# Five edits to the S5 scan stage of a one-core mixer kernel: scan tables, a fourth input buffer, a pinned state copy

## The chip, the cores and the metric

The kernel runs on one core of one Trainium2 chip. The metric is device time in microseconds (us) of that core, taken as the median over runs. Three runs of the kernel before gave 2406.51, 2410.03 and 6112.23 us; their median is 2410.03 us. The profile that is read below comes from one further execution, which took 2415.59 us.

## The reference, cut to what matters

The program is one inference step of a two-layer backbone over 2048 latent tokens and 128 context tokens (2176 together), width 1024. Layer 0 has two branches, gated linear attention and a bidirectional S5 state-space branch. Only the S5 branch is touched here. For each of 32 groups of 16 channels it runs a complex linear recurrence with 64 states, forward and backward in time, adds a skip term and applies a gelu:

```python
def s5_scan(u, lam_re, lam_im, log_dt, b_re, b_im, h0_re, h0_im):
    ...
    bu_re = jnp.einsum('blgh,gph->blgp', u, bb_re)
    bu_im = jnp.einsum('blgh,gph->blgp', u, bb_im)
    ...                                   # the start state h0 enters at token 0
    _, _, h_re, h_im = lax.associative_scan(combine, (a_re, a_im, bu_re, bu_im), axis=1)
    return h_re, h_im
# in even_mixer, forward and flipped, then
y5 = einsum(h_re, c_re) - einsum(h_im, c_im) + s5_d * uf
z = jax.nn.gelu(y5)
```

The final states of the context pass are an output too.

## The kernel before, in words

**Stages.** The kernel runs an input projection for part of the columns (`phase1`), then the S5 core woven with a dense projection (`s5_core` with `qz_pass`), then the S5 output gate with the backward half of the linear attention, the attention chunks, and the second layer. The change lies in the S5 core, which runs from about 286 to 705 us of the span.

**The S5 core.** The 2176 tokens are cut into 136 blocks of 16. A group g passes through three functions. `first(g)` loads its rows of a Toeplitz matrix (`tz`, by DMA on SP's queue), prepares small tables on ScalarE (ACT) and VectorE (DVE), and has GpSimd (POOL) build the weights `e`. `second(g)` transposes the input on TensorE (PE) into `U` (evicted by ACT, lines 694 to 696), transposes `e` into `winc` (702, 704), multiplies both into the block increments (708), and then runs the recurrence over blocks on DVE: lines 714 to 717 rotate the increments with the cosine and sine tables C and S, line 722 is one real scan per direction whose multiplicand is `go` (a decay per state, with zeros where the sequences meet), and lines 723 to 726 rotate back into H. `third(g)` copies the final state out of H (`s5fin`, line 731), multiplies U and H into the output on PE (735 to 738), applies the gelu on ACT (`zy`, 740) and stores it by two DMAs on ACT's queue (742).

**The tables.** `tables(g0)` serves the two groups g0 and g0+1. It copies 16 start columns on ACT (626 to 628) and doubles their length three times (m = 16, 32, 64): at each level four scalings on ACT (`tabw`, 637) and eight multiply-adds on DVE (641). The next level needs the result of the level before, so ACT and DVE hand over to each other three times. `tabs` has two buffers, so the tables of one pair can be written once the pair two before has been used up (its last reader is line 725). `go` is written by two ACT instructions for each group (675) into a ring of three buffers, U lies in a ring of three, which are zeroed at their edges by nine POOL memsets in `s5_setup` (396).

**The dense work.** Between the steps of the core, `qz_pass` gives PE blocks of 24 matmuls (100 to 102) into PSUM tiles named psD, of which there are two. ACT evicts each block (`fo`, line 814) and stores it by a DMA on its queue (815). As long as neither psD tile has been evicted, PE cannot begin the next block.

**What sets the order.** Each engine works off its queue in order. The order is written when the kernel is built, by a scheduler that plays the program on modelled durations: among the instructions whose inputs are there in the model, the one that stands first in the program text goes first. A tile whose buffers are all in use waits in the model for the release. The loop of the core is

```python
for g in range(33):
    if g < 27: weights(g + 5)
    if g < 31: first(g + 1)
    if g < 32: second(g)
    yield            # one dense block
    if g: third(g - 1)
    yield            # one dense block
```

Of the kernel before, what the change touches and what calls it, by code (L numbers as in the profile page):

```python
# [14 lines left out]
F32 = mybir.dt.float32  # L15
# [4 lines left out]
AF = mybir.ActivationFunctionType  # L20
# [28 lines left out]
class Kernel:  # L49
# [317 lines left out]
    def s5_setup(self, es):  # L367
# [24 lines left out]
        self.s5_U = []  # L392
        for j in range(3):
            u = c.tile([128, 2, 139], F32, name=f"s5U{j}")
            for z in (0, 129, 138):
                nc.gpsimd.memset(u[:, :, z : z + 1], 0.0)
            self.s5_U.append(u)
        V, G = nc.vector, nc.gpsimd
        with ExitStack() as e2:
            p = self.pool(e2, "s5s", 1, side="left")  # L400
            n = [0]
# [163 lines left out]
    def s5_core(self, es):  # L565
# [48 lines left out]
        late = self.pool(es, "s5l", 1, side="left")  # L614

        def tables(g0):

            t = p.tile([128, 2, 2, 2, 138], F32, name="tabs", tag="tabs", bufs=2)
            AA, BB = self.s5_AA, self.s5_BB
            for d in range(2):  # L620
                dg = slice(d * 32 + g0, d * 32 + g0 + 2)

                at = (lambda m, n: slice(m, m + n)) if d == 0 else (lambda m, n: slice(129 - m - n, 129 - m))
                rev = (lambda n: slice(0, n)) if d == 0 else (lambda n: slice(n - 1, None, -1))
                e = 128 if d == 0 else 0
                nc.scalar.copy(t[:, :, d, :, at(0, 16)], BB[:, :, dg, rev(16)].rearrange("p c g n -> p g c n"))
                nc.scalar.copy(t[:, :, d, :, e], AA[:, :, dg, 8].rearrange("p c g -> p g c"))
                nc.scalar.copy(t[:, :, d, :, 129:138], BB[:, :, dg, rev(9)].rearrange("p c g n -> p g c n"))
            four = [(d, gg) for d in range(2) for gg in range(2)]
            for m in (16, 32, 64):  # L630

                turn = lambda j, d, gg: AA[:, j, d * 32 + g0 + gg, m // 16 : m // 16 + 1]
                at = lambda d, a: slice(a, a + m) if d == 0 else slice(129 - m - a, 129 - a)
                ws = []
                for d, gg in four:
                    ws.append(p.tile([128, 2, 64], F32, name="tabw", tag="tabw", bufs=6)[:, :, 0:m])
                    nc.scalar.activation(ws[-1], t[:, gg, d, :, at(d, 0)], AF.Copy, scale=turn(1, d, gg))  # L637
                for (d, gg), w in zip(four, ws):
                    for j, op in ((0, OP.subtract), (1, OP.add)):
                        x = t[:, gg, d, j]  # L640
                        V.scalar_tensor_tensor(x[:, at(d, m)], x[:, at(d, 0)], turn(0, d, gg), w[:, 1 - j], op0=OP.mult, op1=op)  # L641
            return t
# [3 lines left out]
        quad, tabs, es, tzs, Hs, gos = {}, {}, {}, {}, {}, {}  # L646

        def first(g):
# [22 lines left out]
            if g % 2 == 0:  # L671
                tabs[g // 2] = tables(g)
            go = gos[g] = p.tile([128, 2, 138], F32, name="rgo", tag="rgo", bufs=3)
            for d in range(2):
                nc.scalar.activation(go[:, d], self.s5_go[:, d], AF.Copy, scale=self.s5_m16[:, d * 32 + g : d * 32 + g + 1])
# [11 lines left out]
        def second(g):  # L687

            ug, ut = quad[g // 4]
            U = self.s5_U[g % 3]  # L690
# [18 lines left out]
            C, S = (tabs[g // 2][:, g % 2, :, j] for j in range(2))  # L709
            go = gos.pop(g)  # L710
# [17 lines left out]
        def third(g):  # L728

            U, H, tz, ct = self.s5_U[g % 3], Hs.pop(g), tzs.pop(g), cts.pop(g)  # L730
            nc.scalar.copy(self.s5_fin[:, :, g], H.rearrange("p d c -> p (d c)")[:, 137:268:130])
# [8 lines left out]
            nc.scalar.activation(zy, py, AF.Gelu_apprx_tanh)  # L740
            for kt in range(2):
# [1057 lines left out]
```

## Time and profile before

| what | value |
|---|---|
| median of the runs | 2410.03 us |
| the profiled execution | 2415.59 us |
| its span, first to last instruction | 2413.7 us |
| mean granted TensorE clock over the span | 0.966 |
| PE busy over the span | 2268.3 us (94%) |
| DVE busy | 1659.3 us (69%) |
| ACT busy | 1042.7 us (43%) |
| POOL busy | 867.6 us (36%) |

The span is the time from the first to the last instruction; the profiled execution's own time is 1.9 us longer. PE, DVE, ACT and POOL are the four engines; PEld is PE's loading of weights, ACTq and SPq are the DMA issues on the queues of ACT and SP. An `L` with a number is a line of the kernel. In a row of waits, the instruction on the left had to wait for the one on the right of the arrow. In a row of the timeline, the bracket says how long the engine had been idle before the instruction and what ended that wait. The granted clock (PEclk) is 1.00 at 2.4 GHz and 0.50 at 1.2 GHz.

### The profile page before, as it was taken

How to read it: one execution, taken by the hardware profiler on the slowest of the kernel's cores; microseconds unless marked ns; L12 is line 12 of the kernel's file. 1: busy time of each engine (PE TensorE's matmuls, PEld its weight loads, DVE VectorE, ACT ScalarE, POOL GpSimd, SP SyncE). 2: the span in 40 equal slices, each digit the busy share in tenths (PEclk: the TensorE clock that was granted, in tenths of full speed). 3: DMA queues.
4: the chain of work that ended last, by engine and by line, in shares of the span. 5: the costliest groups of instructions: out<-in, count | busy, mean ns of one | idle time of the engine just before them, and what ended most of it. 6: DMA issues, size and time to landing. Idle time of an engine off the chain costs nothing.

```text
span 2413.7 us, 47276 instructions
## 1 busy us (share of the span) xinstructions
PE 2268.3 (94%) x17473; PEld 2108.3 (87%) x17473; DVE 1659.3 (69%) x3916; ACT 1042.7 (43%) x2533; POOL 867.6 (36%) x1348
## 2 busy tenths in 40 slices
PE   7999887888899987999999999999999997999998
PEld 4988787887897876888888999999999997999998
DVE  4997688888866776888887665565344336676765
ACT  3554644343544453455454432233122115565653
POOL 4127165566522227767674021111101102222221
PEclk9999988999999995999999999999999998999999
DMA  9765853343469873333333642245133223222221
GB/s 322 236 210 181 252 162 99 102 132 110 131 212 310 291 232 100 123 119 123 116 115 102 210 120 80 80 138 147 50 93 102 68 69 100 88 89 88 90 69 58
DMA packets 328040, 332.90 MB, mean 138 GB/s; under 512 B 43969, under 2 KB 274977, under 8 KB 327809
## 3 DMA queue, kind: packets, MB, share of 16 engines
q1 hardware_dynamic: 265312, 238.84, 33.1%
q0 software_dynamic: 14384, 48.65, 5.9%
q10 hardware_dynamic: 48112, 42.38, 5.4%
q8 instruction: 138, 2.26, 0.4%
q14 instruction: 94, 0.76, 0.1%
HBM read 223.57 MB, written 106.22 MB: 137 GB/s over the span
## 4 chain that ended last, share of the span: by engine, by line
PE 57%; DVE 8%; issue 4%; DMA 4%; ACT 2%; POOL 2%; SPq 0%; ACTq 0%; POOLq 0%; DVEq 0%
PE psD L100 7%; PE psW L100 7%; PE psW L101 7%; PE psW L102 7%; PE psD L102 7%; PE psD L101 7%; PE psP L1081 3%; PE psW L1510 2%; PE psW L1463 2%; DVE tabs L641 2%; PE psT L1498 2%; PE psP L1098 1%; PE psP L1096 1%; DMA wst<-in_w_in_o_dram 1%; DMA wst<-h_d 1%
## 5 line engine op out<-in xcount | busy, mean ns | idle before, releaser
L100 PE MATMUL psD<-slot,yT 128*128 128x256 f32 x1088 | 318.2, 293 | 1.9 <-ACT yT L1125 1.9
L102 PE MATMUL psD<-slot,yT 128*128 128x256 f32 x1088 | 314.1, 292 | 0.0
L101 PE MATMUL psD<-slot,yT 128*128 128x256 f32 x1088 | 310.7, 286 | 0.0
L101 PE MATMUL psW<-hq,slot 128*128 128x272 f32 x1024 | 293.0, 287 | 0.0
L102 PE MATMUL psW<-hq,slot 128*128 128x272 f32 x1024 | 292.9, 287 | 0.0
L100 PE MATMUL psW<-hq,slot 128*128 128x272 f32 x1024 | 289.1, 287 | 0.0
L100 PE MATMUL psD<-hq,slot 128*128 128x272 f32 x768 | 235.1, 308 | 46.8 <-ACT fo L814 45.8
L101 PE MATMUL psD<-hq,slot 128*128 128x272 f32 x768 | 230.0, 300 | 0.0
L102 PE MATMUL psD<-hq,slot 128*128 128x272 f32 x768 | 229.5, 300 | 0.0
L100 PEld LDWEIGHTS psD<-slot,yT 128*128 128x128 f32 x1088 | 208.1, 191 | 10.0 <-ACT yT L1125 2.0
L102 PEld LDWEIGHTS psD<-slot,yT 128*128 128x128 f32 x1088 | 205.8, 191 | 4.5 <-issue 2.2
L101 PEld LDWEIGHTS psD<-slot,yT 128*128 128x128 f32 x1088 | 208.1, 191 | 1.8
L100 PEld LDWEIGHTS psD<-hq,slot 128*128 128x128 f32 x768 | 151.8, 199 | 55.2 <-ACT fo L814 48.8
L102 PEld LDWEIGHTS psW<-hq,slot 128*128 128x128 f32 x1024 | 193.1, 189 | 0.0
L101 PEld LDWEIGHTS psW<-hq,slot 128*128 128x128 f32 x1024 | 192.5, 188 | 0.0
L100 PEld LDWEIGHTS psW<-hq,slot 128*128 128x128 f32 x1024 | 190.6, 188 | 0.0
L641 DVE SCALAR_TENSOR_TENSOR tabs<-tabs,s5A,tabw 128x16 f32<-128x16 f32 (+2 forms) x384 | 146.8, 447 | 24.9 <-ACT tabw L637 23.5
L101 PEld LDWEIGHTS psD<-hq,slot 128*128 128x128 f32 x768 | 152.1, 198 | 6.4 <-issue 4.7
L102 PEld LDWEIGHTS psD<-hq,slot 128*128 128x128 f32 x768 | 152.1, 198 | 1.0 <-issue 1.0
L1472 DVE CUSTOM_DVE_ANT_0 sc<-psW,amask,sink 128x512 f32<-128x512 f32 (+1 forms) x128 | 93.6, 732 | 84.7 <-PE psT L1498 76.2
L1007 ACT ACTIVATE arg<-arg 128x512 f32<-128x512 f32 x119 | 75.0, 631 | 143.6 <-POOL arg L1006 140.3
L1475 ACT ACTIVATE sc<-sc,nm 128x512 f32<-128x512 f32 (+1 forms) x128 | 90.9, 710 | 87.9 <-DVE nm L1474 74.8
(376 smaller groups left out, 6543.2 us busy)
## 6 DMA issues: line engine op xcount, KB each, us to landing
wst<-h_d SPq DMA_DIRECT2D x96, 272.0 KB
hq<-hl_d SPq DMA_DIRECT2D x40, 544.0 KB
hl_d<-ht POOLq DMA_DIRECT2D x17, 1024.0 KB, 6.7
wada<-in_w_ada_dram SPq DMA_DIRECT2D x32, 512.0 KB
h_d<-hf SPq DMA_DIRECT2D x17, 512.0 KB
x_d<-x ACTq DMA_DIRECT2D x17, 512.0 KB
h_d<-hf ACTq DMA_DIRECT2D x17, 512.0 KB
wst<-h_d SPq DMA_DIRECT2D x34, 256.0 KB
```

What stands on the lines that cost most here:

```text
L100: mm(out, lh, rh, start=start, stop=False)
L101: mm(out, lh, rl, start=False, stop=False)
L102: mm(out, ll, rh, start=False, stop=stop)
L641: V.scalar_tensor_tensor(x[:, at(d, m)], x[:, at(d, 0)], turn(0, d, gg), w[:, 1 - j], op0=OP.mult, op1=op)
L1007: nc.scalar.activation(arg, arg, AF.Exp, scale=0.0625)
L1081: nc.tensor.matmul(pv[:, hh, pr, :], ak[o : o + 64, pr, :], aq[o : o + 64, pr, :], start=True, stop=True)
L1096: nc.tensor.matmul(ot, qh[o : o + 64, 0, pr, :], sf[o : o + 64, pr], start=True, stop=False)
L1463: nc.tensor.matmul(out, r32(qs[:, j, h]), kk, start=j == 0, stop=j == 1)
L1472: V.tensor_tensor_reduce(sv, ps, mask, 1.0, sk[:, h : h + 1], op0=OP.add, op1=OP.max, accum_out=m)
L1475: nc.scalar.activation(sv, src, AF.Exp, bias=nm[:, h : h + 1], accum_out=sm[:, h : h + 1])
L1498: nc.tensor.transpose(pt[:, c, :], t[:, 128 * c : 128 * c + 128], self.ident)
L1510: nc.tensor.matmul(po[kv][:, j % 2], r32(VV[:, b, kv]), r32(t[:, x, :, c, :]), start=c + x == 0, stop=c + x == nb)
```

## The change

Five edits, all in the S5 core. (1) The tile of the tables gets a third plane that holds `go` for its pair of groups, written in `tables` by four ACT instructions ahead of the doubling; the ring of `go` buffers is gone. (2) `tables(g + 1)` is called in `first(g)` of odd g instead of `tables(g)` in `first(g)` of even g, so each call stands one group earlier in the program. (3) U has four buffers instead of three; they and their memsets move from `s5_setup` to the core. (4) The copy of the final state stands behind the gelu, and is pinned there: `keep_in_program_order` lets the scheduler put it on ACT's queue only behind the ACT instruction that stands before it in the program, which is the gelu. (5) `tabw` has four buffers instead of six.

```diff
-        self.s5_U = []
-        for j in range(3):
-            u = c.tile([128, 2, 139], F32, name=f"s5U{j}")
-            for z in (0, 129, 138):
-                nc.gpsimd.memset(u[:, :, z : z + 1], 0.0)
-            self.s5_U.append(u)
@@ s5_core
         late = self.pool(es, "s5l", 1, side="left")
+        self.s5_U = []
+        for j in range(4):
+            u = late.tile([128, 2, 139], F32, name=f"s5U{j}")
+            for z in (0, 129, 138):
+                nc.gpsimd.memset(u[:, :, z : z + 1], 0.0)
+            self.s5_U.append(u)
@@ tables
-            t = p.tile([128, 2, 2, 2, 138], F32, name="tabs", tag="tabs", bufs=2)
+            t = p.tile([128, 2, 2, 3, 138], F32, name="tabs", tag="tabs", bufs=2)
...
+            for d, gg in four:
+                j = d * 32 + g0 + gg
+                nc.scalar.activation(t[:, gg, d, 2], self.s5_go[:, d], AF.Copy, scale=self.s5_m16[:, j : j + 1])
...
-                    ws.append(p.tile([128, 2, 64], F32, name="tabw", tag="tabw", bufs=6)[:, :, 0:m])
+                    ws.append(p.tile([128, 2, 64], F32, name="tabw", tag="tabw", bufs=4)[:, :, 0:m])
@@ first
-            if g % 2 == 0:
-                tabs[g // 2] = tables(g)
-            go = gos[g] = p.tile([128, 2, 138], F32, name="rgo", tag="rgo", bufs=3)
-            for d in range(2):
-                nc.scalar.activation(go[:, d], self.s5_go[:, d], AF.Copy, scale=self.s5_m16[:, d * 32 + g : d * 32 + g + 1])
+            if g == 0:
+                tabs[0] = tables(0)
+            if g % 2 and g < 31:
+                tabs[g // 2 + 1] = tables(g + 1)
@@ second
-            U = self.s5_U[g % 3]
+            U = self.s5_U[g % 4]
...
-            C, S = (tabs[g // 2][:, g % 2, :, j] for j in range(2))
-            go = gos.pop(g)
+            C, S, go = (tabs[g // 2][:, g % 2, :, j] for j in range(3))
@@ third
-            U, H, tz, ct = self.s5_U[g % 3], Hs.pop(g), tzs.pop(g), cts.pop(g)
-            nc.scalar.copy(self.s5_fin[:, :, g], H.rearrange("p d c -> p (d c)")[:, 137:268:130])
+            U, H, tz, ct = self.s5_U[g % 4], Hs.pop(g), tzs.pop(g), cts.pop(g)
...
             nc.scalar.activation(zy, py, AF.Gelu_apprx_tanh)
+            self.tc.keep_in_program_order(nc.scalar.copy(self.s5_fin[:, :, g], H.rearrange("p d c -> p (d c)")[:, 137:268:130]))
```

## Rows read from the trace of the kernel before

**Rows 1.** Busy time by engine in two stretches: the S5 core, what follows.

```profile
300.00:705.00 405.00, 348.80 (x2588) 329.08 (x2587) 332.66 (x757) 175.19 (x594) 229.97 (x331) 0.92 0.44 130
705.00:755.00 50.00, 47.06 (x346) 40.11 (x345) 29.87 (x58) 26.85 (x62) 11.38 (x19) 0.97 1.00 303
```

**Rows 2.** Waits in 290 to 705 us: total us, times, longest us.

```profile
ACT tabw L637 <- DVE tabs L641: 59.8, 67, 4.0
PE psD L100 <- ACT fo L814: 45.8, 13, 5.6
ACT s5U L696 <- PE psW L736: 43.8, 14, 4.8
ACT s5fin L731 <- DVE rh L726: 41.3, 28, 4.3
DVE ra L714 <- PE psW L708: 32.1, 11, 4.8
ACT rgo L675 <- DVE rb L722: 25.7, 12, 5.1
```

**Rows 3.** Timeline of PE: five short stalls of the dense blocks.

```profile
394.94 0.39 PE L100 MATMUL psD<-hq,slot 128*128 128x272 f32 x1 [2.74 <-ACT fo L814]
...
448.14 0.39 PE L100 MATMUL psD<-hq,slot 128*128 128x272 f32 x1 [2.57 <-ACT fo L814]
...
500.09 0.39 PE L100 MATMUL psD<-hq,slot 128*128 128x272 f32 x1 [3.02 <-ACT fo L814]
...
551.68 0.39 PE L100 MATMUL psD<-hq,slot 128*128 128x272 f32 x1 [3.02 <-ACT fo L814]
...
605.09 0.39 PE L100 MATMUL psD<-hq,slot 128*128 128x272 f32 x1 [2.55 <-ACT fo L814]
```

**Rows 4.** Timeline of PE: five long stalls, the first and the last.

```profile
366.56 0.59 PE L100 MATMUL psD<-hq,slot 128*128 128x272 f32 x1 [5.63 <-ACT fo L814]
...
577.85 0.59 PE L100 MATMUL psD<-hq,slot 128*128 128x272 f32 x1 [5.53 <-ACT fo L814]
```

**Rows 5.** Timeline of ACT around the short stall of 448 us, and after it.

```profile
447.39 0.41 ACT L675 ACTIVATE rgo<-s5go,s5m 128x138 f32<-128x138 f32 x1 [4.37 <-DVE rb L722]
447.71 0.38 ACT L814 ACTIVATE fo<-psD 128x272 f32<-128x272 f32 x1
...
453.54 0.21 ACT L696 COPY s5U<-ugt 128x16 f32<-128x16 f32 x1 [3.23 <-PE psW L736]
454.00 0.40 ACT L740 ACTIVATE zy<-psW 128x274 f32<-128x274 f32 x1 [0.26 <-PE psW L738]
```

**Rows 6.** Timeline of ACT before the long stall that ends at 472.75 us.

```profile
459.16 0.20 ACT L731 COPY s5fin<-rh 128x2 f32<-128x2 f32 x1 [2.33 <-DVE rh L726]
...
460.00 0.71 ACT L675 ACTIVATE rgo<-s5go,s5m 128x138 f32<-128x138 f32 x2
...
470.58 0.73 ACT L637 ACTIVATE tabw<-tabs,s5A 128x128 f32<-128x128 f32 x2 [1.78 <-DVE tabs L641]
...
472.30 0.40 ACT L814 ACTIVATE fo<-psD 128x272 f32<-128x272 f32 x1 [0.99 <-DMA z_d<-zy]
```

**Rows 7.** Timeline of DVE in the same stretch.

```profile
457.42 0.77 DVE L725 TENSOR_TENSOR ra<-rb,tabs 64x276 f32<-64x276 f32 x1
...
460.95 6.97 DVE L641 SCALAR_TENSOR_TENSOR tabs<-tabs,s5A,tabw 128x16 f32<-128x16 f32 x12 [1.82 <-ACT tabw L637]
467.84 0.43 DVE L714 TENSOR_TENSOR ra<-tabs,psW 128x276 f32<-128x276 f32 x1
```

**Rows 8.** Busy time by engine right after that long stall (columns as in rows 1).

```profile
472.70:478.20 5.50, 5.45 (x25) 5.45 (x26) 3.15 (x10) 1.94 (x6) 0.00 (x0) 0.53 0.21 67
```

**Rows 9.** Views of two tiles, tabs and s5U: one line of each.

```profile
L641 DVE SCALAR_TENSOR_TENSOR tabs<-tabs,s5A,tabw x384: 220/275/1274, 288.4 to 672.5; 128x16 f32<-128x16 f32 x64, 128x32 f32<-128x32 f32 x64, 128x64 f32<-128x64 f32 x64
...
L396 POOL MEMSET s5U<- x9: 101/101/103, 65.5 to 65.8; 128x2 f32 x9
```

**Rows 10.** The smallest form of line 641, in 300 to 705 us.

```profile
L641 DVE SCALAR_TENSOR_TENSOR tabs<-tabs,s5A,tabw 128x16 f32<-128x16 f32 x120 | 57.3, 544 | 23.4 <-ACT tabw L637 23.3
```

In rows 1 and 8 the columns are the stretch and its length, then busy us (and instructions) of PE, PEld, DVE, ACT and POOL, the granted clock, the share of the DMA engines and GB/s. In rows 9 stand the count, min/median/max ns of one instruction, the first and last start, and the forms; in rows 10 busy us, mean ns of one, and the idle time before them.

More of the change, by code (lines that the diff above doesn't have):

```diff
@@ L625, in tables @@
                 e = 128 if d == 0 else 0
-                nc.scalar.copy(t[:, :, d, :, at(0, 16)], BB[:, :, dg, rev(16)].rearrange("p c g n -> p g c n"))
-                nc.scalar.copy(t[:, :, d, :, e], AA[:, :, dg, 8].rearrange("p c g -> p g c"))
-                nc.scalar.copy(t[:, :, d, :, 129:138], BB[:, :, dg, rev(9)].rearrange("p c g n -> p g c n"))
+                nc.scalar.copy(t[:, :, d, 0:2, at(0, 16)], BB[:, :, dg, rev(16)].rearrange("p c g n -> p g c n"))
+                nc.scalar.copy(t[:, :, d, 0:2, e], AA[:, :, dg, 8].rearrange("p c g -> p g c"))
+                nc.scalar.copy(t[:, :, d, 0:2, 129:138], BB[:, :, dg, rev(9)].rearrange("p c g n -> p g c n"))
             four = [(d, gg) for d in range(2) for gg in range(2)]
+            for d, gg in four:
+                j = d * 32 + g0 + gg
+                nc.scalar.activation(t[:, gg, d, 2], self.s5_go[:, d], AF.Copy, scale=self.s5_m16[:, j : j + 1])
             for m in (16, 32, 64):
@@ L635, in tables @@
                 for d, gg in four:
-                    ws.append(p.tile([128, 2, 64], F32, name="tabw", tag="tabw", bufs=6)[:, :, 0:m])
-                    nc.scalar.activation(ws[-1], t[:, gg, d, :, at(d, 0)], AF.Copy, scale=turn(1, d, gg))
+                    ws.append(p.tile([128, 2, 64], F32, name="tabw", tag="tabw", bufs=4)[:, :, 0:m])
+                    nc.scalar.activation(ws[-1], t[:, gg, d, 0:2, at(d, 0)], AF.Copy, scale=turn(1, d, gg))
                 for (d, gg), w in zip(four, ws):
@@ L645, in s5_core @@
         up = self.u_d[NLAT:NT, :].rearrange("(c t) (g h) -> c g t h", t=16, h=16)
-        quad, tabs, es, tzs, Hs, gos = {}, {}, {}, {}, {}, {}
+        quad, tabs, es, tzs, Hs = {}, {}, {}, {}, {}
         def first(g):
```

## The prediction

> **What bounds the kernel now.** I read first the busy times of the S5 core. In 405 us PE is busy for 348.8 and DVE for 332.7, ACT for only 175.2 [rows 1]. So neither PE (56.2 us idle) nor DVE (72.3 us idle) fills the stage, and all that a better order in it can give lies within these two figures. Then I read who waits. PE's idle time is nearly all of one kind: 45.8 us in 13 waits for `fo`, the eviction of a dense block by ACT [rows 2]. ACT is idle for more than half of the stage and still late with it, since it works off its queue in order and stands before instructions whose inputs are missing: `tabw` (59.8 us), the U copy (43.8), the final state's copy (41.3), `go` (25.7) [rows 2]. Last I read the timelines, to see which of these waits stands ahead of an `fo` that PE needs. PE's stalls have two shapes:
>
> - **Short**, five of them, 2.74, 2.57, 3.02, 3.02 and 2.55 us, together 13.90 us [rows 3]. ACT waits 4.37 us for an old scan to release a `go` buffer, and `fo` stands right behind that `go` [rows 5].
> - **Long**, five of 5.5 to 5.6 us [rows 4]. ACT goes through the `tabw` chain, waits 1.78 us for DVE's table work in the midst of it, then 0.99 us behind the gelu's DMA issues, and then comes `fo` [rows 6]. In the 5.5 us after such a stall PE's granted clock is 0.53, the level of 1.2 GHz [rows 8], so about 0.47 x 5.5 = 2.6 us more are lost each time.
>
> After both shapes PE brings the increments late, and DVE waits for them (32.1 us in 11 waits, rows 2). That is the same time seen from another engine, and I do not add it.
>
> **Part by part.**
>
> *`go` moves into the tables.* The 64 instructions stay, and so does their form; the wait for the scan goes. Their new buffer is that of the tables, whose copies wait for line 725 anyway. With the wait, the short stalls go, as `fo` is then first in line: -13.90 us. Bounds: 0, if another late instruction slides in ahead of `fo`; -13.9 at best. What is late next there is `winc`, whose inputs come from PE itself. On the other side, four `go` instead of two stand ahead of each doubling chain. Two take 0.71 us [rows 6], 0.3 to 0.4 each as they overlap, so the chain starts 0.6 us later. Where the chain holds up `fo` (the five long stalls) that costs 5 x 0.6 = +3.0 us.
>
> *The final state's copy behind the gelu.* The copy's wait stands in front of the tables' copies: these need line 725, which ends at 457.42 + 0.77 = 458.19, but the copy runs at 459.16 [rows 6, 7]. So the chain can start 0.97 us earlier, five times: -4.9 us. Behind the gelu the copy finds H long done and costs its 0.2 us. Bounds: 0, if the gelu now waits for H in its place, and -4.9. Together with the two more `go`: -1.9 us.
>
> *Four buffers for U.* ACT's wait for PE's line 736 goes (43.8 us in 14 waits), but behind it stands the gelu, which waits for line 738 of the same `third` and comes 0.26 us after [rows 5]. ACT is held to the same point, and meanwhile PE is busy with those very matmuls. I cost it at nothing; the cover is PE's own work. If the scheduler uses the freedom to bring increments forward, the gain is at most the part of DVE's 32.1 us that is not behind the short stalls, some 18 us; this end goes to the second rival. Twelve memsets instead of nine, at 0.1 us [rows 9], move on POOL's queue from 65 us to the start of the stage, behind POOL's DMA issues of the projection; the first U is written at 300 us. Nothing, or 1.2 us once if they come late.
>
> *Tables a group ahead.* They still have two buffers, and the copies already run within 2 us of the release: line 725 ends at 458.19, the `go` that follow the copies start at 460.00 [rows 6, 7]. Earlier in the program is therefore not earlier in time. What changes is rank: table work now comes before the `second` that it used to follow. In the long shape DVE ran lines 714 to 716 (three of 0.43 us) between twelve and twelve multiply-adds of the chain [rows 7], and ACT's wait of 1.78 us lay there. If the chain goes first, `fo` comes 1.3 us earlier five times, -6.5 us; if the modelled order stays, 0. I take half, -3.2.
>
> *`tabw` from six to four.* A level uses four, and each scaling of the next level needs the multiply-adds that free its predecessor's buffer. Nothing; where two tables overlap, at the start, one level's handover of four times the mean wait (59.8/67 = 0.9 us) or 3.6 us, once.
>
> *Given back.* POOL's 230 us of work then fall into a shorter stage, and DVE's multiply-adds are slow beside POOL: the smallest form takes 544 ns in the mean where the shortest took 220 [rows 9, 10]. A stage shorter by 18 us raises POOL's share from 57 to 59.5 in a hundred; if the further 2.5 in a hundred of DVE's 332.7 us ran at half pace, 8 us would be added, of which I take a quarter as on the path: +2.0 us, bounds 0 and 8.
>
> The Trainium skill says more on this (SBUF — State Buffer, section "Who interferes with whom"): a DVE instruction with two SBUF inputs and a GpSimd instruction that reads SBUF exclude each other, the later one blocking fully. By that rule the stage would be full already and the sum would be zero. The trace agrees only in part: DVE finished twelve multiply-adds in 6.97 us, and a full block would let none through beside a busy POOL. It stands as the first rival below.
>
> **Sum.** -13.9 - 1.9 - 3.2 + 2.0 = -17.0 us. Against the profiled execution (2415.6 us) that is 2398.6. This execution lies 5.6 us above the median of the runs (2410.0), so the median becomes **2393 us**. What follows the core is PE-bound at 47.1 of 50 us [rows 1], so I carry the gain to the end undiminished.
>
> **Rivals.**
>
> *The slack is taken up by DVE and POOL.* The waits leave ACT, but DVE's own chain lengthens as its work falls beside POOL's. For it: 544 against 220 ns. Against it: DVE is idle for 72 us. The give-back is then at its upper bound and the table terms at zero: -13.9 + 8 = -6, or 2404 us.
>
> *All of `fo`'s lateness goes.* With three of its four waits removed, ACT comes to every `fo` in time: 45.8 us, and 5 x 2.6 = 13 us of clock, -59 us, within DVE's 72.3 idle us: about 2352 us. Against it: the `tabw` wait, the greatest, is not touched. Half of the way is as likely as all of it, so I put this case at 2352 to 2375.
>
> *Slower: every pair takes the long shape.* With the tables ranked before `second`, ACT puts the whole chain, now with four `go`, ahead of `winc` and `fo` in both pairs of four groups, instead of in every other one. It decides from the point where `fo` stands behind the last `tabw` in the pairs that now have the short shape. Each short stall of 2.8 us becomes 5.5 + 2.6 = 8.1: 5 x 5.3 = +26.5 us, or 2437 us. With the remaining six of the 16 pairs at 8.1 too it would be +75 and 2485. For it: the wait on line 725 stays at the chain's head. Against it: of the chain itself nothing changes but its start, by 0.6 us.
>
> *The edits change nothing.* The tables are bound by their buffers, the U copy by the gelu, and another wait slides ahead of `fo`: 2410. This is near the first rival, and I count the two together.
>
> **How the numbers follow.** Forecast 0.52 (its own range, from the terms' bounds, 2380 to 2404), first rival with no change 0.23 (2402 to 2414), all lateness gone 0.12, slower 0.13. For 8 in 10 the range runs from 2358, which keeps about half of the good case, to 2428, which leaves out most of the slow one. The measurement tells about 2%, here 48 us, from no change. Faster by more than that (under 2362) needs most of the good case: 0.09. Slower by more (over 2458) needs the slow one in nearly all pairs: 0.05. The rest, 0.86, lies within.
>
> **What would show it.** Right: no wait for the scan in ACT's list any more; no stall of 2.5 to 3 us of PE on `fo`; waits for H gone from the state's copy, with the gelu's own wait for line 738 grown; the U copy no longer waiting for line 736; the `tabw` wait still near 60 us, and long stalls of about 5 us with a clock near 0.5 behind them. Wrong: more than ten stalls of PE on `fo`; a stage whose PE idle time stays at 56 us though the scan wait is gone; DVE's busy time in the stage above 340 us; an ACT wait on line 725 that has grown by what the others lost.

## The result, and the profile after

Four runs of the changed kernel have a median of 2384.03 us (2383.14 to 2391.86), three of the kernel before beside them 2410.03 (2406.51 to 2414.85). Two runs, one of the kernel before (6112.23 us) and one of only_pin below (3555.09), were in a much slower state and are in no median here. The ratio is 0.9888, 95% interval 0.9869 to 0.9907: faster by 26 us between the medians, 27 by the ratio, or 1.1%, which by the bound of 2% counts as within it. The forecast was 2393. It lay 9 us too high.

I cut both traces at the same four events: ACT's first write to a table, the transpose of the final state on PE (end of the core), the first matmul into psP (end of the next stage), and ACT's first `asq` (end of the third). All stages between these follow by name. The core took 417.6 us and takes 396.3 (-21.3), the next stage 198.9 and now 191.3 (-7.6), the third 472.4 and 470.9, the rest 1039.0 and 1037.3; the core starts 1.1 us later. The four differences and the start give the 30.9 us by which the span is shorter (2413.7 to 2382.8).

Busy time by engine of the kernel before, then of the changed kernel, in the core and in the next stage (columns as in rows 1):

```profile
285.89:703.53 417.64, 355.96 (x2633) 335.62 (x2631) 340.76 (x779) 187.97 (x630) 229.97 (x331) 0.92 0.46 134
...
703.53:902.43 198.90, 189.61 (x1420) 157.01 (x1417) 137.06 (x287) 99.64 (x231) 51.26 (x89) 0.99 0.85 274
```

```profile
286.97:683.31 396.34, 350.59 (x2656) 333.00 (x2655) 338.63 (x781) 182.82 (x634) 240.09 (x331) 0.93 0.48 142
683.31:874.60 191.29, 180.29 (x1396) 153.29 (x1393) 136.00 (x286) 98.01 (x228) 51.94 (x92) 0.99 0.88 285
```

In the core PE's idle time went from 61.7 to 45.8 us. The count of PE's instructions is the second thing to see: 23 more in the core, 24 fewer behind it. By tile they are 24 matmuls of a dense block (`psD` from `hq`), which the scheduler has drawn from the next stage into the core. So the two stages are best taken as one sum: 616.5 us before, 587.6 after, with 4053 and 4052 instructions. At the pace of the next stage before (189.6 us busy for 1420 instructions) the 24 are worth some 3.2 of its 7.6 us; this is an estimate.

Waits of the changed kernel in 280 to 690 us, which answer to [rows 2]:

```profile
ACT zy L740 <- PE psW L738: 62.8, 24, 9.3
...
ACT tabs L626 <- DVE ra L726: 30.9, 12, 7.6
...
ACT tabw L640 <- DVE tabs L644: 27.6, 31, 5.5
...
PE psW L737 <- DVE rh L727: 25.3, 10, 4.4
ACT s5U L698 <- PE psW L736: 24.9, 12, 5.4
PE psD L100 <- ACT fo L815: 9.0, 3, 6.1
DVE ra L715 <- PE psW L710: 7.5, 5, 3.0
```

Two waits of the kernel before that belong beside these, in 290 to 705 us:

```profile
ACT zy L740 <- PE psW L738: 11.6, 17, 3.1
...
ACT tabs L626 <- DVE ra L725: 4.9, 5, 1.5
```

PE's wait for `fo` has fallen from 45.8 to 9.0 us, and in its place stands a wait that the kernel before hardly had (0.5 us): 25.3 us for `H`, the result of the scans. ACT's waits for the scan and for `H` are gone, the gelu's has grown from 11.6 to 62.8, `tabw` has halved, and the tables' copies now wait 30.9 us for line 726 (the line 725 of before, 4.9 us there).

Timelines of the changed kernel, DVE first, then ACT, PE and POOL, in the stretch that answers to [rows 6, 7]:

```profile
398.37 6.61 DVE L644 SCALAR_TENSOR_TENSOR tabs<-tabs,s5A,tabw 128x16 f32<-128x16 f32 x22 [1.54 <-ACT tabw L640]
404.90 0.43 DVE L715 TENSOR_TENSOR ra<-tabs,psW 128x276 f32<-128x276 f32 x1
...
409.04 1.67 DVE L723 TENSOR_TENSOR_SCAN rb<-tabs,ra 128x138 f32<-128x138 f32 x2
...
411.46 0.44 DVE L725 TENSOR_TENSOR ra<-rb,tabs 64x276 f32<-64x276 f32 x1
...
412.39 0.45 DVE L727 TENSOR_TENSOR rh<-rh,ra 128x276 f32<-128x276 f32 x1
...
416.16 0.87 DVE L725 TENSOR_TENSOR ra<-rb,tabs 64x276 f32<-64x276 f32 x1
```

```profile
398.03 0.94 ACT L640 ACTIVATE tabw<-tabs,s5A 128x32 f32<-128x32 f32 x4
...
399.62 0.39 ACT L815 ACTIVATE fo<-psD 128x272 f32<-128x272 f32 x1
...
402.27 0.38 ACT L815 ACTIVATE fo<-psD 128x272 f32<-128x272 f32 x1
...
403.10 0.41 ACT L640 ACTIVATE tabw<-tabs,s5A 128x128 f32<-128x128 f32 x1
...
416.03 0.40 ACT L740 ACTIVATE zy<-psW 128x274 f32<-128x274 f32 x1 [9.32 <-PE psW L738]
```

```profile
412.89 0.82 PE L737 MATMUL psW<-rh,ct 128*128 128x137 f32 x2 [4.44 <-DVE rh L727]
```

```profile
399.25 1.26 POOL L577 TENSOR_TENSOR ct<-s5M,s5CY 128x272 f32<-128x272 f32 x2
402.94 1.32 POOL L578 TENSOR_TENSOR ct<-s5R,s5CX 128x272 f32<-128x272 f32 x2 [2.43 <-PE psW L738]
...
409.62 1.52 POOL L577 TENSOR_TENSOR ct<-s5M,s5CY 128x272 f32<-128x272 f32 x2
416.08 1.46 POOL L578 TENSOR_TENSOR ct<-s5R,s5CX 128x272 f32<-128x272 f32 x2 [4.93 <-PE psW L738]
```

Before, DVE did twelve multiply-adds of a chain, then `second`'s products, then the other twelve [rows 7]. Now it does 22 of the 24 first. Over the 16 passes, the five that were cut after twelve now run 24, 22, 24, 24 and 24 in a row; most of the others are still cut. ACT's chain of scalings takes 5.5 us (398.03 to 403.51), where it took 10.7 (460.61 to 471.31). One `fo` stood in the midst of the chain before, two stand in this one.

The chain needs the first 16 of the 24 multiply-adds, as the last eight, of its third level, feed no scaling. Busy time from the first to the end of the 16th (columns as in rows 1), in the kernel before, the changed one, and two kernels of the next section, only_ahead and ahead_u4:

```profile
460.95:470.81 9.86, 6.26 (x52) 6.04 (x51) 9.80 (x20) 3.70 (x13) 9.49 (x15) 1.00 0.14 42
```

```profile
398.37:402.43 4.06, 4.06 (x36) 4.06 (x35) 4.06 (x17) 3.56 (x13) 2.14 (x4) 1.00 0.08 30
```

```profile
403.39:408.23 4.84, 4.84 (x43) 4.84 (x42) 4.84 (x17) 3.87 (x15) 3.14 (x6) 1.00 0.02 8
```

```profile
454.67:462.24 7.57, 7.57 (x65) 7.56 (x63) 7.57 (x17) 4.24 (x15) 6.96 (x12) 1.00 0.18 56
```

So the 16 took 9.86 us with POOL busy for 9.49 of them, and now take 4.06 with POOL busy for 2.14: it pauses for 2.43 us, until PE's line 738 frees a buffer of `ct`. Of the 5.8 us between the two only 1.3 are the three products that no longer lie in between. The rest is that the multiply-adds themselves are shorter, as they are in few_pool below, where POOL has little to do.

But `second`'s products wait behind the 22, the scans behind the products, and PE stands 4.44 us for `H` at 412.89. The granted clock behind this stall is 0.50, the level of 1.2 GHz, as it was 0.53 behind a long stall of before [rows 8]:

```profile
412.80:418.30 5.50, 5.41 (x24) 5.41 (x25) 5.21 (x12) 0.48 (x2) 2.22 (x3) 0.50 0.17 49
```

### The profile page after: what moved, and what is told of

Same layout as the page of the kernel before. It is cut to its first block, busy times and chain, and to the rows that moved or that the text cites. A ratio compares the mean times of both kernels' runs of the same rounds, so it can differ in the third digit from the quotient of the medians.

```text
span 2382.8 us, 47320 instructions
## 1 busy us (share of the span) xinstructions
PE 2251.9 (95%) x17473; PEld 2101.3 (88%) x17473; DVE 1656.2 (70%) x3916; ACT 1035.6 (43%) x2533; POOL 879.1 (37%) x1351
## 3 DMA queue, kind: packets, MB, share of 16 engines
q1 hardware_dynamic: 265312, 238.84, 33.4%
## 4 chain that ended last, share of the span: by engine, by line
PE 61%; DVE 11%; DMA 4%; issue 4%; ACT 3%; POOL 2%; ACTq 0%; SPq 0%; POOLq 0%; DVEq 0%
PE psD L100 8%; PE psD L102 7%; PE psD L101 7%; PE psW L100 7%; PE psW L102 7%; PE psW L101 7%; DVE tabs L644 3%; PE psP L1082 3%; PE psW L1511 3%; PE psW L1464 2%; PE psT L1499 2%; PE psP L1099 1%; PE psP L1097 1%; DVE rb L723 1%; DMA wst<-in_w_in_o_dram 1%
## 5 line engine op out<-in xcount | busy, mean ns | idle before, releaser
L100 PE MATMUL psD<-hq,slot 128*128 128x272 f32 x768 | 232.6, 303 | 18.1 <-ACT fo L815 9.0
L102 PE MATMUL psD<-hq,slot 128*128 128x272 f32 x768 | 227.4, 296 | 0.0
L101 PE MATMUL psD<-hq,slot 128*128 128x272 f32 x768 | 226.7, 296 | 0.2 <-DVE hq L232 0.2
L100 PEld LDWEIGHTS psD<-slot,yT 128*128 128x128 f32 x1088 | 207.6, 191 | 10.7 <-ACT yT L1126 2.4
L100 PEld LDWEIGHTS psD<-hq,slot 128*128 128x128 f32 x768 | 149.7, 195 | 24.6 <-ACT fo L815 9.6
L101 PEld LDWEIGHTS psD<-hq,slot 128*128 128x128 f32 x768 | 149.5, 195 | 4.0 <-issue 3.5
L102 PEld LDWEIGHTS psD<-hq,slot 128*128 128x128 f32 x768 | 149.4, 195 | 2.5 <-issue 2.5
L644 DVE SCALAR_TENSOR_TENSOR tabs<-tabs,s5A,tabw 128x16 f32<-128x16 f32 (+2 forms) x384 | 117.6, 374 | 28.6 <-ACT tabw L640 27.4
```

What stands on the lines that cost most here:

```text
L100: mm(out, lh, rh, start=start, stop=False)
L101: mm(out, lh, rl, start=False, stop=False)
L102: mm(out, ll, rh, start=False, stop=stop)
```

## Experiments

One table for all. Times are medians; the ratio is to the kernel before, run beside each on the same chip (its medians there were 2409.0 to 2411.3 us); "two stages" is the core and the next one in the profiled execution; "chain" is the time from the first to the last `tabw` scaling, summed over the 16 passes of the tables.

| kernel | us | ratio, interval | core | two stages | third | PE on `fo` | PE on `H` | chain |
|---|---|---|---|---|---|---|---|---|
| before | 2410.03 | 1 | 417.6 | 616.5 | 472.4 | 45.8 | 0.5 | 153.6 |
| only_pin | 2401.90 | 0.9969 (0.9958 to 0.9981) | 413.3 | 604.6 | 474.0 | 41.6 | under 0.5 | 158.1 |
| only_u4 | 2403.09 | 0.9972 (0.9961 to 0.9982) | 406.8 | 602.8 | 471.4 | 37.7 | 1.1 | 151.3 |
| only_go | 2393.24 | 0.9935 (0.9923 to 0.9947) | 404.2 | 601.7 | 468.9 | 31.9 | 8.1 | 157.1 |
| only_ahead | 2391.55 | 0.9928 (0.9915 to 0.9941) | 390.8 | 587.6 | 481.3 | 11.5 | 21.1 | 133.2 |
| no_ahead | 2387.02 | 0.9894 (0.9878 to 0.9911) | 402.8 | 593.6 | 469.9 | 33.0 | 2.9 | 168.8 |
| no_go | 2385.02 | 0.9891 (0.9876 to 0.9906) | 397.7 | 589.7 | 472.4 | 18.1 | 17.3 | 139.2 |
| no_pin | 2390.59 | 0.9914 (0.9899 to 0.9929) | 390.6 | 586.1 | 480.2 | 9.5 | 26.0 | 122.9 |
| no_u4 | 2381.40 | 0.9883 (0.9868 to 0.9898) | 395.2 | 584.9 | 471.4 | 9.5 | 24.6 | 122.9 |
| ahead_pin | 2382.76 | 0.9898 (0.9880 to 0.9917) | 397.3 | 588.2 | 471.1 | 14.3 | 14.5 | 142.0 |
| ahead_u4 | 2404.25 | 0.9983 (0.9972 to 0.9993) | 409.2 | 605.6 | 471.1 | 42.5 | 1.8 | 137.6 |
| fin_dve | 2394.54 | 0.9950 (0.9934 to 0.9966) | 396.8 | 591.8 | 480.4 | 7.1 | 25.3 | 117.8 |
| few_pool | 2325.59 | 0.9661 (0.9647 to 0.9676) | 343.7 | 535.9 | 471.4 | 4.2 | 0.2 | 97.2 |
| after | 2384.03 | 0.9888 (0.9869 to 0.9907) | 396.3 | 587.6 | 470.9 | 9.0 | 25.3 | 119.5 |

The cores rank roughly by PE's wait for `fo`, not by the chain: no_ahead has the longest chain (168.8) and a core of 402.8, ahead_u4 a shorter one (137.6) and 409.2.

**Each edit by itself.** The kernel before with one edit of the diff. `tabw` is cut to four buffers only where the larger tables or the fourth U need the room.

only_go:

```diff
-            t = p.tile([128, 2, 2, 2, 138], F32, name="tabs", tag="tabs", bufs=2)
+            t = p.tile([128, 2, 2, 3, 138], F32, name="tabs", tag="tabs", bufs=2)
...
-            go = gos[g] = p.tile([128, 2, 138], F32, name="rgo", tag="rgo", bufs=3)
```

> The kernel before with one edit: go lies in the tables (third plane, four instructions ahead of the doubling), tabw has four buffers; the tables stand where they stood. Theory A (the wait for an old scan's go buffer was the stall that counted): the five short stalls of 2.5 to 3 us go, the long ones of 5.5 us stay; PE's wait on fo falls from 45.8 to about 32 us and the time by 12 to 17 us (ratio 0.993 to 0.995). Theory B (the rank of the tables ahead of second removed the long stalls, and this is most of the gain): under 8 us. Theory C (any edit makes the scheduler write another order, and the 27 us are what that order happens to give): anything between -30 and +20 us, with stalls at other places.

The core is shorter by 13.4 us and the time by 16.7. The short stalls between the long ones shrink to 0.2 to 0.6 us, five long ones of 4.1 to 5.4 us stay. The term for `go` (-13.9) had its size right.

only_ahead:

```diff
-            if g % 2 == 0:
-                tabs[g // 2] = tables(g)
+            if g == 0:
+                tabs[0] = tables(0)
+            if g % 2 and g < 31:
+                tabs[g // 2 + 1] = tables(g + 1)
```

> The kernel before with one edit: each call of tables stands one group earlier. Theory A: the two table buffers set the start of the copies, so nothing moves in time; within 4 us of before, short and long stalls both there. Theory B: DVE does the table chain before the second that used to stand ahead of it, the long stalls go (27.7 us of PE and 13 us of its clock): 15 to 25 us faster. Theory C: anything, with stalls at other places.

The two stages together take 587.6 us, just what they take in the full change: -28.9. The forecast had put -3.2 on this edit; theory B's 15 to 25 us is what came. DVE's timeline shows whole passes of 24 multiply-adds with nothing between, in every second pass of the steady part:

```profile
403.39 10.30 DVE L641 SCALAR_TENSOR_TENSOR tabs<-tabs,s5A,tabw 128x16 f32<-128x16 f32 x24 [0.61 <-ACT tabw L637]
...
450.76 10.29 DVE L641 SCALAR_TENSOR_TENSOR tabs<-tabs,s5A,tabw 128x16 f32<-128x16 f32 x24 [0.61 <-ACT tabw L637]
```

```profile
ACT tabw L637 <- DVE tabs L641: 37.5, 44, 3.8
ACT rgo L677 <- DVE rb L724: 33.4, 11, 5.6
...
PE psW L739 <- DVE rh L728: 21.1, 10, 3.7
...
PE psD L100 <- ACT fo L816: 11.5, 4, 4.2
```

In the waits of 290 to 700 us the one for the scan (33.4 us) is longer than before, and still PE waits for `fo` only 11.5 us: no stall of PE on `fo` falls behind this wait in the timeline. Behind the four longest of these waits PE stands for `H`, which comes of the same scans. So the row that went with 13.9 us of stalls on `fo` before goes with none here. The time gains less than the two stages (18.4 us), as the third takes 481.3 us instead of 472.4.

only_pin:

```diff
-            nc.scalar.copy(self.s5_fin[:, :, g], H.rearrange("p d c -> p (d c)")[:, 137:268:130])
...
             nc.scalar.activation(zy, py, AF.Gelu_apprx_tanh)
+            self.tc.keep_in_program_order(nc.scalar.copy(self.s5_fin[:, :, g], H.rearrange("p d c -> p (d c)")[:, 137:268:130]))
```

> The kernel before with one edit: the final state's copy stands behind the gelu and is pinned there. Theory A: ACT's wait for H (41.3 us) goes, the tables' copies start about 1 us earlier, 2 to 5 us faster; the scan wait and the short stalls stay. A rival (the copy's wait held up every fo behind it): 10 us or more faster. Theory C: anything.

The core is shorter by 4.3 us (the term said -4.9), though it holds 23 of the 24 dense matmuls more; with the next stage the gain is 11.9. The time falls by 8.0. Five long stalls of 4.9 to 5.6 us stay.

only_u4:

```diff
-        for j in range(3):
+        for j in range(4):
-            u = c.tile([128, 2, 139], F32, name=f"s5U{j}")
+            u = late.tile([128, 2, 139], F32, name=f"s5U{j}")
```

> The kernel before with one edit: four buffers for U in the core's pool, tabw with four. Theory A: the gelu waits for the same matmuls, so within 4 us of before; ACT's wait of 43.8 us for line 736 turns into a wait of the gelu for line 738. A rival (a third group of increments can be prepared, so DVE no longer waits for PE): 8 to 18 us faster. Theory C: anything.

The core is shorter by 10.8 us, the time by 6.9, where the forecast said nothing; that lies between theory A's 4 and the rival's 8. The short stalls are down to some 2.2 us, the long ones to 5.1, and the order of the core is another on all queues.

The four gains in time, 16.7 + 18.4 + 8.0 + 6.9, sum to 50 us, the whole change gives 26 to 27. They are not four parts of one sum.

**Each edit taken back.** The changed kernel without one edit.

no_ahead:

```diff
-            if g == 0:
-                tabs[0] = tables(0)
-            if g % 2 and g < 31:
-                tabs[g // 2 + 1] = tables(g + 1)
+            if g % 2 == 0:
+                tabs[g // 2] = tables(g)
```

> The changed kernel with one edit undone: the calls of tables stand where they stood before. Theory B2 (formed on the single edits: standing ahead, the tables take the long stalls of 5 us away; go in the tables takes the short ones): the long stalls of 5 us on fo come back, PE's wait on fo rises from 9 to 25 to 35 us, and the S5 core is 8 to 15 us longer than with the whole change; the time 8 to 15 us above the changed kernel's 2384. Theory A (the go ring was what counted): within 4 us of the changed kernel.

The long stalls are back (PE waits 33.0 us for `fo`, `tabw` 63.8), the two stages are longer by 5.9 us, the time by 1 (by the ratios) to 3 us, within the intervals. The 8 to 15 us that were expected did not come, as the core is longer by only 6.4. So the other edits, too, reach most of the gain without this one.

no_go:

```diff
+            go = gos[g] = p.tile([128, 2, 138], F32, name="rgo", tag="rgo", bufs=3)
+            for d in range(2):
+                nc.scalar.activation(go[:, d], self.s5_go[:, d], AF.Copy, scale=self.s5_m16[:, d * 32 + g : d * 32 + g + 1])
```

> The changed kernel with one edit undone: go stays in its own ring of three buffers, written group by group. Theory B2: with the tables ahead ACT's wait for the scan comes back (25 to 35 us), but the alone standing edit of the tables had already left only 11.5 us of PE's wait on fo with that ring: the S5 core within 4 us of the changed kernel. Theory A: the short stalls of 2.5 to 3 us come back, the core 12 to 16 us longer.

ACT's wait for the scan is back with 37.3 us in 13, and the two stages lose 2.1 us, the time 1. Once the tables stand ahead, `go` in them is worth next to nothing.

no_pin:

```diff
-            self.tc.keep_in_program_order(nc.scalar.copy(self.s5_fin[:, :, g], H.rearrange("p d c -> p (d c)")[:, 137:268:130]))
```

(The copy stands ahead of the matmuls of `third` again.)

> The changed kernel with one edit undone: the final state's copy stands at the head of third again, free. Expected by both theories: ACT waits for H at the copy again (25 to 40 us) and the gelu's wait for line 738 shrinks by about as much; the core 0 to 6 us longer. By a rival (the pin only moves the wait): no longer at all.

ACT waits 64.7 us for `H` at the copy, and 27.4 instead of 62.8 at the gelu: the pin moves a wait, and the two stages take 586.1 us, 1.5 less. As the rival had it, the core is no longer (390.6). The time is longer by 6 us, all of it in the third stage (480.2).

no_u4:

```diff
-        for j in range(4):
-            u = late.tile([128, 2, 139], F32, name=f"s5U{j}")
+        for j in range(3):
+            u = c.tile([128, 2, 139], F32, name=f"s5U{j}")
```

> The changed kernel with one edit undone: three buffers for U, set up early as before. Theory A and B2: within 4 us of the changed kernel, as the gelu waits for the same matmuls. A rival (the fourth buffer lets PE prepare a group more): the core 6 to 12 us longer, with DVE's wait for line 708 (710) up from 7.5 to some 20 us.

ACT's wait of the U copy for line 736 is 71.2 us in 20, the gelu's only 15.0, and time and stages are those of the change or a little less (2381.4). The gelu behind it is held to the same point, as the forecast had it. In the core PE, DVE and POOL work in the very order of the changed kernel, so there the fourth buffer buys nothing.

**Order against mechanism.** After these eight I compared the order of the instructions on each queue. All kernels with the next stage in the changed kernel's order (after, only_pin, no_go, no_u4) took 189.7 to 192.0 us for it, those in the order of before (before, only_ahead, only_u4) 196.0 to 198.9; the other three, each in an order of its own, lie between 190.8 and 197.5. The third stage took 469.9 to 472.4 us in the order that before, after, only_u4, no_u4 and no_ahead share, and 481.3 and 480.2 in one that only_ahead and no_pin share. None of the lines of these stages is edited. For the next stage a rival stands beside the order, and no run here parts the two: how many matmuls the core has left to it. All kernels with 1385 to 1393 matmuls started there, whatever the order, took 189.7 to 192.2 us, and all with 1409 to 1416 took 195.0 to 198.9. The third stage has no such difference in its counts. Three kernels tested the order with it known ahead of the run.

ahead_pin: the kernel before with the edits of only_ahead and only_pin together.

> The kernel before with tables a group ahead and the state's copy pinned, the rgo ring and three buffers for U as before. All stages behind the core stand on every queue in the changed kernel's order, the core in another. Order theory: the stage behind the core takes 189.5 to 192.5 us and the next 470 to 473, as in every kernel with these orders; the core by the single edits 390.8 less at most 4.3, up to 397.7 (the version with all edits but the rgo planes); time 2375 to 2388. Rival, that the length of the stage behind the core follows from what the core leaves behind (the kernel with tables ahead alone had 196.8 and 481.3): 195 or more and 480, time 2390 or more.

The next stage takes 190.9 us, the third 471.1, the time is 2382.76: all three as the order theory had them (the count of matmuls, 1393, says the same of the first), and two of the edits give the whole gain.

ahead_u4: the kernel before with the edits of only_ahead and only_u4 together.

> The kernel before with tables a group ahead and four buffers for U; no pin, the rgo ring as before. All stages behind the core stand in the order of the kernel before. Order theory: the stage behind the core takes 195 to 199 us and the next 470 to 473, though tables stand ahead as in the changed kernel; core 380 to 392 (390.8 with the tables alone); time 2373 to 2389. Rival, the gain behind the core belongs to tables that stand ahead: 190 to 192 us there. If the core is above 394, a fourth buffer for U costs where the tables stand ahead.

196.4 and 471.1 us behind the core, as the order said. The core was missed: 409.2 us instead of at most 392. Rows of DVE, PE, ACT, and ACT's wait for the scan in 290 to 700 us:

```profile
454.67 7.57 DVE L641 SCALAR_TENSOR_TENSOR tabs<-tabs,s5A,tabw 128x16 f32<-128x16 f32 x16 [0.68 <-ACT tabw L637]
462.16 0.43 DVE L716 TENSOR_TENSOR ra<-tabs,psW 128x276 f32<-128x276 f32 x1
```

```profile
441.70 0.59 PE L100 MATMUL psD<-hq,slot 128*128 128x272 f32 x1 [4.21 <-ACT fo L816]
...
464.93 0.39 PE L100 MATMUL psD<-hq,slot 128*128 128x272 f32 x1 [2.46 <-ACT fo L816]
```

```profile
439.49 0.71 ACT L677 ACTIVATE rgo<-s5go,s5m 128x138 f32<-128x138 f32 x2 [4.89 <-DVE rb L724]
```

```profile
ACT rgo L677 <- DVE rb L724: 41.7, 15, 5.2
```

Two things differ from only_ahead. The `fo` of the stall at 441.70 stands behind `go`, which waits 4.89 us for the scan, as in the short stalls of before. And the chain is longer: DVE does the 16 multiply-adds that it needs without a break, but with POOL busy for 6.96 of their 7.57 us, where only_ahead had 3.14 of 4.84. The chain takes 8.4 us (10.7 before, 5.8 in only_ahead), and the stall behind it is 2.46 us. So both shapes return, 42.5 us on `fo`. Neither the edit nor the unbroken 16 gives the gain by itself; what POOL does beside them counts as well. Why a fourth U brings this order, with the tables ahead, stays open.

fin_dve:

```diff
-            self.tc.keep_in_program_order(nc.scalar.copy(self.s5_fin[:, :, g], H.rearrange("p d c -> p (d c)")[:, 137:268:130]))
+            nc.vector.tensor_copy(self.s5_fin[:, :, g], H.rearrange("p d c -> p (d c)")[:, 137:268:130])
```

> The changed kernel with the final state's copy on DVE, 32 copies of 128x2 more there, none on ACT and nothing pinned. In the core the orders of ACT (but for the copies), POOL and SP are those of the changed kernel, DVE's has the 32 copies in it. Theory that the pinned copy, standing behind the gelu, costs the core the 5.7 us by which it is shorter without the pin (390.6 against 396.3): the core goes to 389 to 392, and gelu waits as long as now (62.8 us). Rival, that DVE's chain to H sets the core: 32 copies of some 0.1 us come into it, core 396 to 400. The stage behind the core is in another order than the changed kernel's, near that of the version without the pin: 195 to 198 us by the order theory, and the one after it near 480; sum 2386 to 2394. If instead it takes 190 to 192 us, that order does not set its length.

The core, 396.8 us, is in the rival's range: ACT without the copies is worth nothing here. That the 32 copies in DVE's chain cost the rest was argued and is not shown, as the core also holds other matmuls. The time, 2394.54, is at the upper end of what was expected. The two stages take 591.8 us, 4.2 more than the change. Behind the core, 195.0 and 480.4 us as the order said. Of the 5.7 us between the cores of no_pin and after, on which the first theory rested, 4.2 come back in the next stage: after holds 22 of the moved dense matmuls more in its core. I saw that only afterwards.

**What bounds the rest.**

few_pool:

```diff
-                G.tensor_tensor(t1, pw(M), cv(self.s5_CY), op=OP.mult)
-                G.tensor_tensor(ct[:, d], ct[:, d], t1, op=OP.add)
...
-                G.tensor_tensor(t1, pw(M), xv(self.s5_Y), op=OP.mult)
-                G.tensor_tensor(e[:, d], e[:, d], t1, op=OP.add)
```

> The changed kernel with two of three POOL operations on ct and e left out: only the product with R is kept, the product with M and their sum are left out, so the values of the S5 core are others and nothing else. It is to show what DVE pays in the core for sharing with POOL. Sharing theory: POOL's 240 us in the core fall to about 80, and with them the DVE means: the 128x16 multiply-adds from 484 ns to at most 350 (their shortest in the kernel before is 220), the scans from 664 ns to about 600; the matmuls' wait for H (25.3 us in 10) falls below 12 and the core from 396 us by 8 or more. Rival, order theory: DVE's means fall as much, but the core is set by the alternation of ACT and DVE on the tables and by the order of the queues, and stays within 4 us of 396. If the means do not fall, POOL is not what makes these instructions long.

The core falls by 52.6 us to 343.7, with a granted clock of 0.99, and PE's wait for `H` to 0.2 us. PE's weight loads wait for POOL's results only 0.7 us in the changed kernel, so it is not that they come earlier. The queues of this kernel stand in an order of their own, so a part of the 52.6 us may be the order's; what DVE gains is read from its own rows. Busy time in the core of few_pool (columns as in rows 1):

```profile
281.00:624.70 343.70, 329.60 (x2663) 316.06 (x2662) 264.60 (x781) 179.34 (x634) 77.75 (x114) 0.99 0.55 164
```

As many instructions of DVE, 781, take 264.6 us instead of 338.6. The groups of DVE, in 283 to 700 us, of the changed kernel and of few_pool (busy us, mean ns of one, idle time before):

```profile
L644 DVE SCALAR_TENSOR_TENSOR tabs<-tabs,s5A,tabw 128x16 f32<-128x16 f32 x128 | 51.4, 468 | 28.3 <-ACT tabw L640 27.4 <-issue 0.9
...
L723 DVE TENSOR_TENSOR_SCAN rb<-tabs,ra 128x138 f32<-128x138 f32 x64 | 39.9, 664 | 1.0
...
L726 DVE TENSOR_TENSOR ra<-rb,tabs 64x276 f32<-64x276 f32 x32 | 23.3, 728 | 0.4
...
L716 DVE TENSOR_TENSOR rb<-tabs,psW 64x276 f32<-64x276 f32 x32 | 14.2, 444 | 0.4
```

```profile
L717 DVE TENSOR_TENSOR_SCAN rb<-tabs,ra 128x138 f32<-128x138 f32 x64 | 42.1, 697 | 1.0
...
L641 DVE SCALAR_TENSOR_TENSOR tabs<-tabs,s5A,tabw 128x16 f32<-128x16 f32 x128 | 21.9, 238 | 24.2 <-ACT tabw L637 23.2 <-issue 0.8
...
L720 DVE TENSOR_TENSOR ra<-rb,tabs 64x276 f32<-64x276 f32 x32 | 15.1, 471 | 0.4
...
L710 DVE TENSOR_TENSOR rb<-tabs,psW 64x276 f32<-64x276 f32 x32 | 14.2, 444 | 0.4
```

The multiply-adds fall from 468 to 238 ns, the products of two SBUF operands from 728 to 471, and the product with an operand in PSUM stays at 444 in both. Only the scans don't fall (664 to 697), which the expectation had wrong; the last section shows what they ran beside.

## Why the prediction was right, and where not

The time lay in the range, and the forecast's case (stalls on `fo` go, part is given back) is what happened. Its sum, -17.0 us, came out as -26.0 between the medians, and the terms were off more than the sum. That the time fell so near owes something to luck: `go` and the pin were priced too high for this company, the tables far too low.

- *`go`, -13.9.* Right for the edit alone (core -13.4), and the sign is there in the changed kernel: no wait for the scan, and no stall of 2.5 to 3 us but one at the core's start (2.72 us at 297.3). Wrong as a term of this sum: beside tables that stand ahead it is worth 2.1 us of the two stages (no_go). The step "with the wait, the short stalls go" took the stalls as belonging to the wait; they belonged to an `fo` right behind it, and another order had none there.
- *Tables a group ahead, -3.2.* The mis-sized step. "What changes is rank" was the right mechanism, priced at 1.3 us per long stall and then halved. It is worth 28.9 us of the two stages by itself. In the changed kernel the five passes that were cut at 12 no longer are, their chains on ACT take 4.9 to 5.7 us instead of 10.7 to 12.1 (119.5 us instead of 153.6 over all 16), and the long stalls go, of which one (6.13 us at 604.54) is left. The signs that I listed as right, "the `tabw` wait still near 60 us, and long stalls of about 5 us", are both wrong: 27.6 us, and that one stall. The 1.3 us of the three products between the halves did come. My error was to take the multiply-adds' own time as given: the 16 that the chain needs fell from 9.4 to 9.7 us of busy time to 5.2 to 5.7 in these passes, as POOL, busy beside all of them before, is busy for half of their time. POOL stood in the forecast only as a cost (+2.0). Nothing in the forecast led to where POOL's pause would fall, so that part of the gain was luck; ahead_u4 is the order in which it falls elsewhere.
- *Pin, -4.9 + 3.0.* About right alone (-4.3). In company taking it away costs the two stages nothing (-1.5): the wait goes to the gelu, as the bound "0, if the gelu now waits for H in its place" had it.
- *Four buffers for U, 0, and `tabw`, 0.* Right in company: no_u4 is the same within the intervals. The sign was half right, 24.9 us of the wait for line 736 are left. Alone the fourth buffer gave 10.8 us of the core, and DVE's wait for the increments, which I had given to the second rival, fell from 32.1 to 19.9; with the tables ahead it lost 18 (ahead_u4 against only_ahead).
- *Given back, +2.0, bounds 0 to 8.* Too small. PE's new wait for `H` is 25.3 us, and 0.2 in few_pool. So it hangs on DVE's time beside POOL, as far as that kernel's other order lets one say, and the first rival's mechanism is real, at three times its price; it came on top of a larger gain and so did not win. By the rule of the Trainium skill (SBUF — State Buffer, section "Who interferes with whom") the sum would have been zero, as a full stage can't gain. What the rule says of the instructions agrees with the rows: those with two SBUF inputs are lengthened, those with a PSUM input are not (444 ns in both kernels). That twelve multiply-adds came through in 6.97 us does not speak against it, as the forecast had it, since POOL's work is single operations with DVE's possible in between. But its full block does not show: behind it a product would lose anything up to a whole POOL operation of 0.7 to 0.9 us, but in the changed kernel 99 of 103 beside POOL take 0.68 to 1.03 us, near twice their 0.444, as if the two took turns; how they share is not shown.
- *"I carry the gain to the end undiminished."* It grew by 7.6 us in the next stage: 24 dense matmuls had moved forward into the core's idle time (some 3.2 us, as estimated above), and the rest stood in another order. Nothing in the profile of before could show that.
- *Signs of being wrong.* One of the four showed in part: ACT's wait on line 725 (now 726) grew from 4.9 to 30.9 us. It took up what the `go` wait lost (25.7), but PE's stalls on `fo` did not follow it.
- Of the slower rival nothing came: the tables did go ahead in the program, but in the passes that had the long shape the chain is half as long, and in the stretch shown two `fo` and `winc` come inside it.

What stays open: how the scheduler comes from these edits to its order. ahead_u4, and the 8 to 10 us more of the third stage in only_ahead, no_pin and fin_dve, show that it decides as much as an edit does.

But for few_pool, which leaves work out, no kernel run beats the change clearly. no_u4 (2381.40) and ahead_pin (2382.76) equal it within their intervals with fewer edits.

## What to carry to other kernels

Where one engine works off a chain of small steps in turns with another, look for what cuts the chain in the other engine's queue, and price the whole of what stands behind the chain's last step, not the piece that lies in the cut, and ask what will run beside the chain in its new place. Gains of edits that all attack one wait are alternatives: take one back at a time before adding them up, and compare stages by their instruction counts, as a scheduler moves work across the cut. And before removing waits, ask which engine's instructions are long because of their neighbour: a core without two of three POOL operations took 52.6 us less, where the five edits took off 21.3.

## What the runs showed of the hardware

Sorted one by one, DVE's products of 276 elements with two SBUF inputs have two durations. In the changed kernel the 52 that ran while POOL stood still took 0.436 to 0.450 us (mean 0.444), the 103 that ran beside a POOL operation (for over 30% of their time) 0.805 in the mean, 99 of them over 0.6. Of the 96 products with an operand in PSUM (lines 715 to 717) 34 ran beside POOL, and all 96 took 0.425 to 0.445. The two rows of line 725 above show one of each: 0.44 us at 411.46, with POOL idle since 411.14, and 0.87 at 416.16, 0.08 us after POOL began. In the kernel before 62 of 159 ran beside POOL (0.798), 97 without (0.442). So 41 more now fall beside POOL, at 0.36 us each: 15 us of DVE's chain to `H`, while the multiply-adds gained 30 (148.7 to 119.1 us). The time beside POOL has moved from the multiply-adds to the products and scans, and DVE's busy time in the core hardly changed (340.8 to 338.6 us). That is the give-back.

The scans have the same two durations, about 0.43 and 0.82 us: 37 of the 64 in the changed kernel are slow, each with POOL busy through all of it, and 27 fast, with POOL busy for 2% of their time. In the kernel before 25 are slow and 39 fast. In few_pool 44 are slow, though POOL is busy for 78 us only; it was busy for 88% of their time. What counts is not how much POOL does but what it does it beside.
